# One MLP column group per layer as seven block products instead of eight

## The chip, the cores and the metric

The kernel runs on one core of one Trainium2 chip. Times are device microseconds of one execution. The engines are named as the profile names them: PE (TensorE, matmuls; PEld its weight loads), DVE (VectorE), ACT (ScalarE), POOL (GpSimd) and SP (SyncE, which here issues the DMAs).

## The reference

An encoder of two layers on a sequence of 256 tokens and 1024 channels. Each layer has a token mixer and then the sub-layer that the change touches, a gated MLP of 2816 channels:

```
a, gval = split(xn @ w_up, 2)          # xn: (256, 1024), w_up: (1024, 2 * 2816)
a = depthwise_conv3(a) + conv_b        # over the tokens
h = h + (gelu(a) * gval) @ w_down      # w_down: (2816, 1024)
```

All inputs are float32. `xn` is the RMS-normalized stream, and a final norm follows the second layer.

## The kernel before

*Products.* Every operand of a float32 product is split in two parts, a high part (a cast to the type that TensorE multiplies fast) and a rest (the operand less its high part); a product is three passes, high by high, high by rest and rest by high. The activations stand in `x2`, split once per sub-layer, channels on the partitions: 8 chunks of 128 channels, for each its two parts and two halves `t` of 128 tokens. They are TensorE's stationary operand; the weights stream as the moving one, 512 columns at a time.

*Weights.* Class `Weights` has a list of loads (1 MB each: 512 rows by 512 columns, or 256 rows of 1024) and a list of pieces, two per load (`raw`, ring of three). `get` returns the next piece and splits ahead: a cast by ScalarE (`wh`, L242) and a rest by VectorE (`wl`, L244), into a ring of five buffers. Inside the MLP, where the order of the instructions is written out by hand (`manual_schedule`, `by_hand`), the piece that is split at `get(i)` is piece i + 4, so its cast waits until TensorE is done with piece i - 1. Between the cast and the rest `run_between` puts what stands in `between`.

*The MLP.* Its columns come in groups of 512: five of the activated branch ("a", 0 to 4), five of the gate ("g", 0 to 4), one of the last 256 columns of both ("b"). A group takes four pieces of 12 matmuls (`by_tokens`: two token halves, two chunks of channels, three passes), or 48. Its result, tokens on the partitions, is turned by `to_z` and `cross`: two transposes by VectorE (L744), a DMA to DRAM, four DMAs back (`reads`, held back behind the next load). Then per pair of 128-channel chunks `steps_up` computes the convolution (six activations by ScalarE at L1405 and L1407, two additions by VectorE at L1411 and L1412), the gelu, the gate (L1419) and the split of the product (L1427, L1428). "d" pieces are rows of `w_down`: one piece is 128 channels by 1024 columns and also takes 12 matmuls (L611 to L613), added up over all 22 chunks in four PSUM banks.

`MLP_GROUPS` is the order of all this. Each piece is a place, counted on from 8 behind the first two groups; `PAIR_PLACES` has, for each of the 11 pairs, the places at which its steps are put between or behind the pieces.

*The norm ahead of the MLP.* `to_channels` scales `h` to `xn`, transposes it by TensorE in groups of four chunks (`xt_ps`), and splits each group by a cast (ScalarE, L528) and a rest (VectorE, L529) into `x2`. GpSimd has only the tiny sums and powers of the norms here (L490 to L495) and, at the start, a small table.

Of the kernel before, what the change touches and what calls it, by code (L numbers as in the profile page):

```python
# [10 lines left out]
F32 = mybir.dt.float32  # L11
F32R = mybir.dt.float32r
# [4 lines left out]
P = 128  # L17
# [9 lines left out]
DFF = 2816  # L27
# [24 lines left out]
SEGMENTS = (HALVES, (slice(0, 512), slice(512, 768), slice(768, D)))  # L52

# [51 lines left out]
class Weights:  # L105
# [8 lines left out]
    def __init__(self, tc, pool, idle, small):  # L114
        self.tc, self.nc, self.pool, self.idle, self.small = tc, tc.nc, pool, idle, small
        self.loads, self.pieces = [], []
        self.n_loaded, self.n_split, self.n_got = 0, 0, 0
        self.raw, self.split = {}, {}
        self.live = set()
        self.behind, self.later = (), []  # L120
        self.last, self.rests = [None, None], {}
        self.between = []
        self.loads_behind = {}
        self.n_scaled, self.gains = 0, None
        self.by_hand, self.held_back = 0, []

    def add(self, src, shape, cuts, tag=None):

# [64 lines left out]
    def _split(self, upto):  # L193
        nc = self.nc
        first = self.n_split
        while self.n_split < len(self.pieces):
            i = self.n_split
            n, cut, shape, slot = self.pieces[i]
            if i >= upto and (slot is None or i >= max(upto, first + 2) or i >= upto + 4 or i < 4):
                break  # L200
            if slot is None and len(self.live) == self.BUFS:
                break
            self.load(n + 1)
            with ExitStack() as queued:
                for insts, some in self.later:
                    for inst in insts if i in some else ():
                        if not self.by_hand:
                            queued.enter_context(self.tc.issue_after(inst.ins))
                for hi, lo, *_ in self.open_next():
                    hi()  # L210
                    self.run_between()
                    lo()
            self.load(self.ahead(i))

    def run_between(self):
# [64 lines left out]
def encoder(ctx, tc, x, w_in, w_pool, pool_scale, w_a, w_b, w_o, norm1, norm2, w_up, conv_w,  # L280
# [22 lines left out]
    def of_both(w, r0, c0):  # L303
# [3 lines left out]
            [src[:, :, g] for g in range(2)], (4, 512), [((lambda t, j=j: t[:, 2 * j : 2 * j + 2, :]), (2, 512)) for j in range(2)]  # L307
        )

    first_up = []  # L310
    for l in range(DEPTH):
        for g in range(NG):
# [26 lines left out]
        first_up.append(len(W.pieces))  # L339
        W.use(up + rows(w_up[l], 512, 4, 0, 512), (("v1",), ("ybig",), ("at2",)))  # L340
        for kind, n in MLP_GROUPS:
            if kind == "b":
# [164 lines left out]
    def to_channels(x2, psum, g):  # L507

        tag = "acc" if psum is acc else "mm"

        def fin(t, r, xn):
            for n in range(4):
                cc = slice(n * 256, (n + 1) * 256)
                normed[t] = nc.vector.scalar_tensor_tensor(
                    out=xn[:, cc], in0=h[:, t, cc], scalar=r[:, 0:1], in1=g[:, cc],
                    op0=ALU.mult, op1=ALU.mult,
                )
            for n in range(2):  # L520
                pt = psum.tile([P, 4, P], F32, tag=tag, name="xt_ps")
                ks = slice(4 * n, 4 * n + 4)
                for k in range(4):
                    c0 = (4 * n + k) * P
                    nc.tensor.transpose(pt[:, k, :], xn[:, c0 : c0 + P], ident)  # L525
                oh, ol = (x2[:, ks, part, t, :] for part in (0, 1))
                last = [
                    nc.scalar.copy(out=oh, in_=pt),  # L528
                    nc.vector.tensor_sub(out=ol, in0=pt, in1=oh.bitcast(F32)),  # L529
                ]  # L530
# [154 lines left out]
    def v_tile():  # L685
        return acc.tile([P, 512], F32, tag="acc", name="v_ps")
# [50 lines left out]
    def cross(rows, y, z, name, but=1, after=None):  # L737
# [3 lines left out]

        with tc.issue_after(after.ins) if after and not W.by_hand else ExitStack():
            for t in range(2):
                nc.vector.transpose(out=y[:, t].rearrange("p q c j -> p c q j"), in_=rows[t])  # L744
# [215 lines left out]
    for l in range(DEPTH):  # L960
# [373 lines left out]
                    made = first[i - 2][1]()  # L1334
        W.by_hand = 0
        x2 = two_parts("x", "x2")
        norm = Norm(to_channels(x2, acc, g2))
        entry = []

        def begin_mlp():  # L1340
# [11 lines left out]

        g1 = gain(norm1[l + 1] if l + 1 < DEPTH else norm_f)

        acth, actl = (
            [
                big.tile([P, n, 2, P], F32R, tag=f"{tag}{j}", name=f"act{tag}{j}")
# [1 line left out]
            ]  # L1359
            for tag in "qk"  # L1360
        )
        acts = {}

        zg = big.tile([P, 2, 8, 4, 32], F32, tag="v1", name="zg")
        zga = big.tile([P, 2, 8, 4, 32], F32, tag="xn", name="zga")
        z_of = {(kind, n): z[:, n % 2] for kind, z in (("g", zg), ("a", zga)) for n in range(NQ)}
        z_of["b", 4 * NQ] = big.tile([P, 8, 4, 32], F32, tag="gates", name="zb")

        def branch(kind, f, count=1):

            n, c = divmod(f, 4)
            z, c = (z_of[kind, n], c) if n < NQ else (z_of["b", 4 * NQ], c + 2 * (kind == "g"))
            return z[:, :, c : c + count].rearrange("p (t a) c j -> p c t a j", t=2)

        def to_z(ps, z, *when):
            y = big.tile([P, 2, 4, 4, 32], F32, tag="v0", name="crossing")
            cross(ps, y, z, "crossing", *when)

        held, ps0 = entry
        ps1 = v_tile()
        for n in range(4):
            v_sum(ps1, x2, 1, n, held[n])
        for i, _ in held:
            W.free(i)
        to_z((ps0, ps1), z_of["a", 0], 2, W.behind[1])

        def steps_up(f):

# [76 lines left out]
        to_z(ps, z_of["g", 0], 0, W.last[1])  # L1467
        with tc.manual_schedule():
            W.by_hand = 1
            place, turn = 8, ()  # L1470
            for kind, n in MLP_GROUPS[1:]:
                ps = None
                for i in range(4):
                    if not between and not behind:
                        break
# [4 lines left out]
                    turn = ()  # L1480
                    place += 1
                if kind != "d":
                    turn = (lambda ps=ps, z=z_of[kind, n]: to_z(ps, z),)
# [40 lines left out]
```

## Time and profile before

| | |
|---|---|
| median of 3 runs | 854.8 us (854.66 to 856.39) |
| profiled execution | 854.74 us, of which its span is 853.0 |
| PE, PEld | 99%, 83% of the span busy, 3925 matmul records |
| DVE, ACT, POOL | 71%, 59%, 4% |
| mean DMA rate | 251 GB/s |

A row of the groups by line gives line, engine, operation, written and read tiles, shape and count, then the busy time in us and the mean of one in ns, then the engine's idle time ahead of these and who ended it. A row of a timeline gives start and length in us. A row of the windows view gives a stretch, its length, and the busy time with the count of instructions for PE, PEld, DVE, ACT and POOL, then the granted clock, the DMA engines' share and GB/s. Matmuls overlap, so their spacing is read from the starts.

### The profile page before, as it was taken

The numbers are of one execution on the slowest core, as the hardware profiler recorded it, in microseconds if no ns is written. First come the engines' busy times: TensorE is split into PE (matmuls) and PEld (weight loads), VectorE is DVE, ScalarE is ACT, GpSimd is POOL, SyncE is SP. The second block draws the span as 40 slices with busy tenths as digits, with TensorE's granted clock in tenths as the row PEclk, the third lists the DMA queues.
The fourth block names the chain that finished last, engine by engine and source line by source line (L and its number), as shares of the span: only waits on it lengthen the run. The fifth ranks groups of instructions, "written<-read, shape, count | busy, mean of one in ns | idle before, by whom it ended". The sixth has DMA issues, their size and how long they took to land.

```text
span 853.0 us, 10910 instructions
## 1 busy us (share of the span) xinstructions
PE 846.1 (99%) x3925; PEld 706.7 (83%) x3925; DVE 606.0 (71%) x794; ACT 501.1 (59%) x727; POOL 34.8 (4%) x96
## 2 busy tenths in 40 slices
PE   9999999999999999999999999999999999999997
PEld 7888888888888888888888888888888888888886
DVE  6958877767766776777755687868577767777674
ACT  7744566654543775758545454577454557566682
POOL 1710000000010000000000000000000100000000
PEclk9999999999999999999999999999999999999999
DMA  8698897796747979997726899768777489898931
GB/s 302 213 304 284 302 287 251 250 295 212 249 179 281 280 258 299 285 297 223 243 102 214 261 281 324 252 224 262 244 261 267 145 288 303 248 287 291 296 141 50
DMA packets 147966, 214.03 MB, mean 251 GB/s; under 512 B 7800, under 2 KB 69184, under 8 KB 147912
## 3 DMA queue, kind: packets, MB, share of 16 engines
q1 hardware_dynamic: 147480, 212.67, 76.6%
q8 instruction: 31, 0.51, 0.2%
q10 hardware_dynamic: 432, 0.66, 0.2%
q14 instruction: 23, 0.19, 0.1%
HBM read 186.02 MB, written 27.28 MB: 250 GB/s over the span
## 4 chain that ended last, share of the span: by engine, by line
PE 98%; DVE 1%; ACT 0%; POOL 0%; issue 0%; DVEq 0%; ACTq 0%; POOLq 0%
PE t_ps L694 64%; PE v_ps L694 6%; PE res_ps L611 6%; PE res_ps L612 6%; PE res_ps L613 6%; PE v_ps L940 3%; PE v_ps L839 1%; PE pool_ps L598 1%; PE o_ps L1223 1%; PE s_ps L1175 1%; PE s_ps L1170 1%; PE o_ps L1219 1%; PE xt_ps L525 1%; PE warm_ps L400 0%; PE xt_ps L790 0%; DVE h L505 0%
## 5 line engine op out<-in xcount | busy, mean ns | idle before, releaser
L244 DVE TENSOR_TENSOR wl<-raw,wh 128x1024 fp32r<-128x1024 f32 x274 | 331.7, 1220 | 157.5 <-ACT wh L242 156.4
L694 PE MATMUL t_ps<-wh,x 128*128 128x512 f32 x1408 | 439.2, 390 | 0.0
L242 ACT CAST wh<-raw 128x1024 fp32r<-128x1024 f32 x274 | 285.0, 1049 | 200.6 <-PE t_ps L694 132.0
L694 PEld LDWEIGHTS t_ps<-wh,x 128*128 128x128 f32 x1408 | 264.3, 188 | 55.0
L694 PE MATMUL t_ps<-wl,x 128*128 128x512 f32 x704 | 273.9, 389 | 0.0
L694 PEld LDWEIGHTS t_ps<-wl,x 128*128 128x128 f32 x704 | 132.2, 188 | 27.2
L613 PE MATMUL res_ps<-wh,actk 128*128 128x512 f32 (+1 forms) x184 | 69.8, 380 | 0.0
L611 PE MATMUL res_ps<-wh,actq 128*128 128x512 f32 (+1 forms) x184 | 69.8, 380 | 0.0
L612 PE MATMUL res_ps<-wl,actq 128*128 128x512 f32 (+1 forms) x184 | 69.7, 380 | 0.0
L694 PE MATMUL t_ps<-wh,po 128*128 128x512 f32 x128 | 41.4, 395 | 0.0
L612 PEld LDWEIGHTS res_ps<-wl,actq 128*128 128x128 f32 x184 | 34.6, 188 | 6.7
L613 PEld LDWEIGHTS res_ps<-wh,actk 128*128 128x128 f32 x184 | 34.6, 188 | 6.6
L611 PEld LDWEIGHTS res_ps<-wh,actq 128*128 128x128 f32 x184 | 34.6, 188 | 6.5
L1407 ACT ACTIVATE a<-zga,prm 128x256 f32<-128x256 f32 x80 | 39.0, 514 | 0.0
L490 POOL TENSOR_SCALAR ss<-ss 128x1 f32<-128x1 f32 x8 | 2.1, 266 | 771.9 <-ACT junk L483 771.9
L694 PEld LDWEIGHTS t_ps<-wh,po 128*128 128x128 f32 x128 | 24.1, 188 | 4.9
L611 PE MATMUL res_ps<-wh,m 128*128 128x512 f32 (+1 forms) x72 | 26.5, 368 | 0.0
L612 PE MATMUL res_ps<-wl,m 128*128 128x512 f32 (+1 forms) x72 | 26.3, 365 | 0.0
L744 DVE STREAM_TRANSPOSE crossing<-t_ps 128x512 f32<-128x512 f32 x40 | 26.1, 691 | 0.0
L613 PE MATMUL res_ps<-wh,m 128*128 128x512 f32 (+1 forms) x72 | 26.0, 366 | 0.0
L694 PE MATMUL v_ps<-wh,x 128*128 128x512 f32 x80 | 25.7, 392 | 0.0
L483 ACT ACTIVATE junk<-h 128x512 f32<-128x512 f32 (+1 forms) x19 | 10.5, 554 | 25.2 <-DVE h L505 25.0
(190 smaller groups left out, 923.6 us busy)
## 6 DMA issues: line engine op xcount, KB each, us to landing
raw<-in_w_in_dram SPq DMA_DIRECT2D x58, 1024.0 KB
raw<-in_w_up_dram SPq DMA_DIRECT2D x40, 1024.0 KB
raw<-in_w_down_dram SPq DMA_DIRECT2D x22, 1024.0 KB
crossing<-crossing SPq DMA_DIRECT2D x22, 512.0 KB
crossing<-way SPq DMA_DIRECT2D x16, 512.0 KB
raw<-in_w_a_dram SPq DMA_DIRECT2D x8, 1024.0 KB
raw<-in_w_o_dram SPq DMA_DIRECT2D x8, 1024.0 KB
zga<-crossing SPq DMA_DIRECT2D x40, 128.0 KB
```

The lines of the kernel that those rows point to most:

```text
L242: inst = nc.scalar.copy(out=h, in_=src)
L244: inst = self.rests[i] = nc.vector.tensor_sub(out=l, in0=src, in1=h.bitcast(F32))
L483: nc.scalar.activation(junk[:, 0 : cc.stop - cc.start], h[:, t, cc], AF.Square, scale=D**-0.5, accum_out=ss[:, n : n + 1],)
L525: nc.tensor.transpose(pt[:, k, :], xn[:, c0 : c0 + P], ident)
L598: nc.tensor.matmul(out, w(k), x, start=(steps is first and k == 0), stop=(steps is last and k == nk - 1), skip_group_check=turns["rest"],)
L611: nc.tensor.matmul(ps, ah, wh, start=first, stop=False, skip_group_check=on)
L612: nc.tensor.matmul(ps, ah, wl, start=False, stop=False, skip_group_check=on)
L613: nc.tensor.matmul(ps, al, wh, start=False, stop=last, skip_group_check=on)
L694: nc.tensor.matmul(ps, x2[:, 2 * n + j, part, t, :], w[:, j, :], start=(n + m == 0), stop=(n == last and m == 5),)
L744: nc.vector.transpose(out=y[:, t].rearrange("p q c j -> p c q j"), in_=rows[t])
L940: nc.tensor.matmul(ps[t], a[:, k, t, :], w[:, j, :], start=(k + m == 0), stop=(k == KD - 1 and m == 2),)
L1407: nc.scalar.mul(out=out, in_=a, mul=row(j, c))
```

## The change

In each layer the groups "a 3" and "g 3" become one entry, "w 3". Its weights are a matrix of 1024 rows by 1024 columns, 512 gate and 512 activated columns. It is cut into four quadrants of 512 by 512 ("11" and "21": gate columns, upper and lower channels; "12" and "22": activated columns), the activations into four blocks (two token halves by two halves of the channels). Seven products of blocks, each 4 chunks by 3 passes or 12 matmuls, give the four result blocks that eight gave before. Four of the products (T1 to T4) have a sum of quadrants as weights:

T1 = "12" - "11", T2 = "22" - T1, T3 = "22" - "12", T4 = "21" - T2.

GpSimd computes these in place in the raw tiles, half a quadrant (128x1024) at a time; they are then split like any piece. The sums of blocks of x that go with them are made once per layer behind the norm: `to_channels` keeps whole copies of its transposes (`xf`), VectorE adds them up and splits them (`sum_x`). What the products have in common is added up in PSUM; three copies by ScalarE and two additions by VectorE move parts between banks.

The 14 pieces of products stand in `BLOCK` between the first 8 "d" pieces, which so far were two entries elsewhere, and the places of the pairs' steps change with them. `SUMS` says behind the split of which piece which differences are issued. The first two quadrants are loaded into the tiles `ybig` and `at2`, which are idle there; "22" and "21" go through the ring of three and stay in it until their last difference is made.

```diff
-    ("g", 0), ("a", 1), ("g", 1), ("d", 0), ("a", 2), ("g", 2), ("a", 3), ("g", 3), ("b", 20),
-    ("a", 4), ("g", 4), ("d", 4), ("d", 8), ("d", 12), ("d", 16), ("d", 20),
+    ("g", 0), ("a", 1), ("g", 1), ("a", 2), ("g", 2), ("w", 3), ("b", 20), ("a", 4), ("g", 4),
+    ("d", 8), ("d", 12), ("d", 16), ("d", 20),
...
-    (11, 14), (14, 16), (19, 22), (23, 26), (31, 34), (35, 38), (40, 42), (44, 46), (51, 54), (56, 58), (53, 56),
+    (11, 14), (14, 16), (19, 22), (21, 23), (46, 48), (49, 51), (52, 54), (58, 60), (61, 63), (64, 66), (66, 68),
...
+BLOCK = (
+    ("11", 0), ("11", 1), "d", ("T1", 0), ("T1", 1), "d", ("22", 0), ("22", 1), "d", ("T2", 0), ("T2", 1), "d",
+    ("21", 0), ("21", 1), "d", ("T3", 0), ("T3", 1), "d", "d", ("T4", 0), ("T4", 1), "d",
+)
+SUMS = {
+    ("11", 0): (("T1", 0),), ("11", 1): (("T1", 1),),
+    ("T1", 0): (("T2", 0), ("T3", 0)), ("T1", 1): (("T2", 1), ("T3", 1)),
+    ("T2", 0): (("T4", 0),), ("T2", 1): (("T4", 1),),
+}
...
+        def sum_of(name, j):
+            at = raw(home[name], j)
+            nc.gpsimd.tensor_sub(out=at, in0=raw(of[name], j), in1=at)
...
+                if whole is not None:
+                    nc.scalar.copy(out=whole[:, t, n], in_=pt)
...
+        def sum_x():
+            a11, a12, a21, a22 = (xf[:, t, n] for t in range(2) for n in range(2))
+            nc.vector.tensor_add(out=a22, in0=a21, in1=a22)
+            nc.vector.tensor_sub(out=a21, in0=a11, in1=a21)
+            nc.vector.tensor_sub(out=a11, in0=a22, in1=a11)
+            nc.vector.tensor_sub(out=a12, in0=a12, in1=a11)
+            s = big.tile([P, 2, 2, 2, 4, P], F32R, tag="m2", name="sx")
+            for t in range(2):
+                nc.scalar.copy(out=s[:, t, :, 0], in_=xf[:, t])
+            for t in range(2):
+                nc.vector.tensor_sub(out=s[:, t, :, 1], in0=xf[:, t], in1=s[:, t, :, 0].bitcast(F32))
...
+            bank_of = {"11": "p", "T1": "t", "22": "t", "T2": "q", "21": "p", "T3": "q", "T4": "q"}
...
+            def products(name, j):
+                i, (wh, wl) = W.get()
+                ps = bank(bank_of[name])
+                passes = [(c, part, w) for c in range(2) for part, w in ((0, wh), (0, wl), (1, wh))]
+                for m, (c, part, w) in enumerate(passes):
+                    nc.tensor.matmul(
+                        ps, operands[name](part, 2 * j + c), w[:, c, :],
+                        start=(name in opens and j + m == 0), stop=(j == 1 and m == 5), skip_group_check=True,
+                    )
+                W.free(i)
```

GpSimd's queue in layer 0, between the norm ahead of the MLP and the norm behind it, held before:

```order
L490 TENSOR_SCALAR ss_2210<-ss_2210 128x1
L492 TENSOR_TENSOR ss_2210<-ss_2210 128x1 x2
L495 TENSOR_TENSOR rstd_2323<-ss_2210,mhalf_77 128x1
L490 TENSOR_SCALAR ss_3668<-ss_3668 128x1
L492 TENSOR_TENSOR ss_3668<-ss_3668 128x1
L495 TENSOR_TENSOR rstd_3767<-ss_3668,mhalf_77 128x1
```

Now, with `raw54` for "11" and the home of T1, T2 and T4, `raw55` for "12" and the home of T3, `raw57` for "22" and `raw59` for "21":

```order
L543 TENSOR_SCALAR ss_2211<-ss_2211 128x1
L545 TENSOR_TENSOR ss_2211<-ss_2211 128x1 x2
L548 TENSOR_TENSOR rstd_2326<-ss_2211,mhalf_77 128x1
L344 TENSOR_TENSOR raw54_2719<-raw55_2725,raw54_2719 128x1024 x2
L344 TENSOR_TENSOR raw54_2719<-raw57_2763,raw54_2719 128x1024
L344 TENSOR_TENSOR raw55_2725<-raw57_2763,raw55_2725 128x1024
L344 TENSOR_TENSOR raw54_2719<-raw57_2763,raw54_2719 128x1024
L344 TENSOR_TENSOR raw55_2725<-raw57_2763,raw55_2725 128x1024
L344 TENSOR_TENSOR raw54_2719<-raw59_2944,raw54_2719 128x1024 x2
L543 TENSOR_SCALAR ss_3769<-ss_3769 128x1
```

Eight subtractions stand where nothing stood; T2 and T3 alternate, and T4 comes last.

VectorE's queue in layer 0 at the group "a 3", before (`wl110` to `wl113` are its four pieces, `wl114` is the first of "g 3"):

```order
L744 STREAM_TRANSPOSE crossing_2878<-t_ps_2788 128x4x4x32
L1411 TENSOR_TENSOR y_2865<-y_2865,a0_2864 128x2x255
L1412 TENSOR_TENSOR y_2865<-y_2865,a2_2866 128x2x255
L244 TENSOR_TENSOR wl110_2876<-raw56_2795,wh110_2875 128x1024
L244 TENSOR_TENSOR wl111_2906<-raw56_2795,wh111_2905 128x1024
L1419 TENSOR_TENSOR g_2924<-y_2865,zg_2378 128x512
L244 TENSOR_TENSOR wl112_2922<-raw57_2832,wh112_2921 128x1024
L1428 TENSOR_TENSOR actk1_2377<-g_2924,actq1_2375 128x512
L244 TENSOR_TENSOR wl113_2944<-raw57_2832,wh113_2943 128x1024
L744 STREAM_TRANSPOSE crossing_2964<-t_ps_2873 128x4x4x32
L744 STREAM_TRANSPOSE crossing_2964<-t_ps_2874 128x4x4x32
L244 TENSOR_TENSOR wl114_2962<-raw58_2886,wh114_2961 128x1024
```

Now, from the rest of the 4th entry of `BLOCK` to that of the 12th (`wl109` and `wl110` are T1, `wl115` and `wl116` T2; `raw56` and `raw58` hold "d" weights):

```order
L258 TENSOR_TENSOR wl109_2885<-raw54_2719,wh109_2884 128x1024
L1509 TENSOR_TENSOR actk1_2427<-g_2887,actq1_2425 128x512
L803 STREAM_TRANSPOSE crossing_2909<-t_ps_2802 128x4x4x32
L803 STREAM_TRANSPOSE crossing_2909<-t_ps_2803 128x4x4x32
L258 TENSOR_TENSOR wl110_2907<-raw54_2719,wh110_2906 128x1024
L258 TENSOR_TENSOR wl111_2925<-raw56_2727,wh111_2924 128x1024
L258 TENSOR_TENSOR wl112_2939<-raw57_2763,wh112_2938 128x1024
L258 TENSOR_TENSOR wl113_2963<-raw57_2763,wh113_2962 128x1024
L258 TENSOR_TENSOR wl114_2974<-raw58_2816,wh114_2973 128x1024
L258 TENSOR_TENSOR wl115_2986<-raw54_2719,wh115_2985 128x1024
L258 TENSOR_TENSOR wl116_3005<-raw54_2719,wh116_3004 128x1024
L258 TENSOR_TENSOR wl117_3016<-raw58_2816,wh117_3015 128x1024
```

The rests now follow each other without the steps of pairs between them, and four of these twelve read a tile that GpSimd writes.

More of the change, by code (lines that the diff above doesn't have):

```diff
@@ L125, in __init__ @@
         self.by_hand, self.held_back = 0, []
+        self.sums = {}
     def add(self, src, shape, cuts, tag=None):
@@ L212, in _split @@
                     lo()
+                if i in self.sums:
+                    self.sums.pop(i)()
             self.load(self.ahead(i))
@@ L743, in cross, with to_blocks, send @@
             for t in range(2):
-                nc.vector.transpose(out=y[:, t].rearrange("p q c j -> p c q j"), in_=rows[t])
+                to_blocks(rows[t], y[:, t])
+        return send(y, z, name, but)
+    def to_blocks(rows, y):
+        nc.vector.transpose(out=y.rearrange("p q c j -> p c q j"), in_=rows)
+    def send(y, z, name, but=1):
         d = dram.tile([2 * P, 4, P], F32, tag=name, bufs=2, name=name)
@@ L1361, in encoder @@
         )
[L1362 to L1387, printed above, removed]
         def steps_up(f):
@@ L1472, in encoder @@
                 ps = None
+                if kind == "w":
+                    for make, after in block_units(n):
+                        at_place(place, make, *turn)
+                        place, turn = place + 1, after
+                    continue
                 for i in range(4):
```

107 lines of the change are left out of this document (102 added, 5 removed).

## The prediction

> **What bounds the kernel now.** I read the page first (span, engine shares, chain), then the groups by line, then the timelines of single engines round the MLP, and last each GpSimd row beside what VectorE did at that moment.
>
> ```profile
> span 853.0 us, 10910 instructions
> PE 846.1 (99%) x3925; PEld 706.7 (83%) x3925; DVE 606.0 (71%) x794; ACT 501.1 (59%) x727; POOL 34.8 (4%) x96
> PE 98%; DVE 1%; ACT 0%; POOL 0%; issue 0%; DVEq 0%; ACTq 0%; POOLq 0%
> ```
>
> The chain that ended last is TensorE for 98% of the span: time is the number of matmuls times their spacing as long as nothing makes TensorE wait. The spacing is read from start to start in TensorE's timeline, since the durations (0.39) overlap. These are the first and the last of the 48 matmuls of the "d 0" entry of layer 0:
>
> ```profile
> 290.32 0.39 PE L611 MATMUL res_ps<-wh,actq 128*128 128x512 f32 x1
> ...
> 300.97 0.39 PE L613 MATMUL res_ps<-wh,actk 128*128 128x512 f32 x1
> ```
>
> 10.65 us over 47 steps is 0.2266 us each. So a usual piece of weights (12 matmuls) lasts TensorE 2.72 us, a piece that is used by one product (6) 1.36 us.
>
> What feeds it, by line, and how busy that was while the two entries ran that the change replaces (a stretch of the windows view; columns PE, PEld, DVE, ACT, POOL):
>
> ```profile
> L244 DVE TENSOR_TENSOR wl<-raw,wh 128x1024 fp32r<-128x1024 f32 x274 | 331.7, 1220 | 157.5 <-ACT wh L242 156.4
> L242 ACT CAST wh<-raw 128x1024 fp32r<-128x1024 f32 x274 | 285.0, 1049 | 200.6 <-PE t_ps L694 132.0
> 323.00:344.70 21.70, 21.70 (x97) 17.98 (x96) 14.57 (x17) 13.43 (x20) 0.00 (x0) 1.00 1.04 297
> ```
>
> A piece costs ScalarE 1.05 (cast) and VectorE 1.22 (rest). ScalarE waits mostly for TensorE to free a buffer, VectorE for ScalarE: both run ahead until the buffers are full. VectorE has 14.6 us of work in 21.7, GpSimd none. The cover is the split's lead: four pieces, 10.9 us.
>
> **The change part by part.**
>
> *Products.* Per layer 96 matmuls become 84. The program's own order counts 24 fewer on TensorE in all, and nothing added: 24 x 0.2266 = 5.4 us off, all of it on the path. Each layer also splits 14 pieces for 16; both engines have room, so that is worth nothing.
>
> *Where the seven products run.* Their 14 pieces stand among 8 pieces of the down projection: 22 units that last TensorE 84 x 0.2266 + 96 x 0.2266 = 40.8 us (counted from 1: T1 is units 4 and 5, T2 10 and 11, T3 16 and 17, T4 20 and 21; units 3, 6, 9, 12, 15, 18, 19 and 22 are "d"). Two product units and one "d" take 5.4 us, in which VectorE must make three rests (3.7), so far well.
>
> *The differences.* Eight GpSimd subtractions of 128x1024 per layer, which no row of this trace shows. The nearest ones:
>
> ```profile
> L443 POOL COPY fsb<-rbt 4x11 f32<-4x11 f32 x1 | 0.2, 188 | 0.0
> L448 POOL COPY fsb<-fsb 4x128 f32<-4x128 f32 x1 | 0.3, 279 | 0.0
> ```
>
> From 11 to 128 elements a copy grows by 91 ns, 0.78 ns an element: 1024 elements with one operand would be 188 + 1013 x 0.78, 1.0 us, the lower end. A second operand fetched after the first makes it 1.8; if the write came in series too it would be 2.6, the upper end. Nothing in the rows decides between the last two; I take the middle, 2.2.
>
> The Trainium skill (GPSIMD Engine Reference, Performance versus the Vector engine) has 4497 ns for such an add of 2048 elements; half of it, 2.25, is an estimate from that page which no run here shows, and the sum below would be 864.5 by it. Its section Engine selection gives elementwise work on two tensors to VectorE, against this change.
>
> *What they meet.* GpSimd's few rows of before say more than their lengths:
>
> ```profile
> 241.50 0.57 POOL L495 TENSOR_TENSOR rstd<-ss,mhalf 128x1 f32<-128x1 f32 x1
> 247.23 1.21 DVE L244 TENSOR_TENSOR wl<-raw,wh 128x1024 fp32r<-128x1024 f32 x1
> 247.41 1.46 POOL L495 TENSOR_TENSOR rstd<-ss,mhalf 128x1 f32<-128x1 f32 x1
> 427.42 0.19 POOL L492 TENSOR_TENSOR ss<-ss 128x1 f32<-128x1 f32 x1 [1.78 <-ACT junk L483]
> 428.99 1.22 DVE L244 TENSOR_TENSOR wl<-raw,wh 128x1024 fp32r<-128x1024 f32 x1
> 429.06 1.21 POOL L492 TENSOR_TENSOR ss<-ss 128x1 f32<-128x1 f32 x1 [1.44 <-ACT junk L483]
> ```
>
> The same tiny instruction takes 0.57 alone and 1.46 when a rest runs; another 0.19 and 1.21. The second ends at 430.27, the rest at 430.21: GpSimd stood still until VectorE's instruction on two SBUF tensors was through. It can last over several such instructions:
>
> ```profile
> L443 POOL COPY fsb<-rbt 4x8 f32<-4x8 f32 x1 | 2.6, 2633 | 0.0
> 28.67 1.41 DVE L255 SCALAR_TENSOR_TENSOR wl<-raw,gcol,wh 128x512 fp32r<-128x512 f32 x2
> 30.00 0.68 DVE L922 TENSOR_TENSOR x<-xu,x 128x512 fp32r<-128x512 f32 x1
> 30.60 0.68 DVE L820 TENSOR_TENSOR xu<-xuh,xul 128x512 f32<-128x512 f32 x1
> ```
>
> A copy of 8 elements lasted 2.63 us over these four. So the two engines take turns at a path to SBUF. The rows show GpSimd waiting; that VectorE waits as long for a difference they can't show, since GpSimd's instructions were all short. I take it to hold both ways.
>
> The Trainium skill (SBUF — State Buffer, SBUF: two separate sides) calls that pair of ports an exclusive lock, held for a whole instruction by whichever began first. Its direction GpSimd-waits agrees with the 1.21 beside 0.19 us above; by its other direction the sum is the forecast's, without it the first rival's.
>
> *The ledger of that path, per layer.* VectorE's other customers of it are the steps of a pair of channel chunks; a transpose holds VectorE, though not the path:
>
> ```profile
> L1412 DVE TENSOR_TENSOR y<-y,a 128x510 f32<-128x510 f32 x22 | 15.2, 692 | 2.3
> L1411 DVE TENSOR_TENSOR y<-y,a 128x510 f32<-128x510 f32 x22 | 14.9, 676 | 12.9 <-ACT y L1405 12.9
> L1419 DVE TENSOR_TENSOR g<-y,zg 128x512 f32<-128x512 f32 x20 | 13.6, 681 | 0.0
> L1428 DVE TENSOR_TENSOR actk<-g,actq 128x512 fp32r<-128x512 f32 x22 | 15.0, 684 | 0.0
> L744 DVE STREAM_TRANSPOSE crossing<-t_ps 128x512 f32<-128x512 f32 x40 | 26.1, 691 | 0.0
> L1407 ACT ACTIVATE a<-zga,prm 128x256 f32<-128x256 f32 x80 | 39.0, 514 | 0.0
> L1405 ACT ACTIVATE y<-zga,prm 128x256 f32<-128x256 f32 x40 | 24.1, 601 | 0.0
> ```
>
> I count from the moment the first difference can start to the moment TensorE reaches unit 12. There is time for: the lead of 10.9, less the first quadrant's own cast and rest (2.3), less the six activations of a pair that ScalarE has ahead of that cast (4 x 0.51 + 2 x 0.60, some 3): 5.6 us; and TensorE's units 1 to 11, eight of 1.36 and three of 2.72: 19.0. Together 24.6 us. In it fall the rests of units 2 to 12 (11 x 1.22 = 13.4), six pair steps (6 x 0.68 = 4.1) and two transposes (1.4, of which half may lie beside a difference: 0.7): 18.2. Six differences are ready in that time too (two T1, two T2, two T3): 6 x 2.2 = 13.2. That is 31.4 of work in 24.6: TensorE waits 6.8 us per layer. At 1.0 a difference it would be nothing, at 1.8 it is 4.4, at 2.6 it is 9.2. Behind unit 12 the remaining two differences, ten rests and five transposes and additions (4.4 + 12.2 + 3.5 = 20.1) fit into TensorE's 21.8. So 13.6 us for two layers, of which the 5.4 pay a part.
>
> Who waits: a T unit's cast stands in ScalarE's queue behind nothing but its difference, so the casts behind it wait as well, and with them VectorE's rests; and the third load of "d" weights on SP's queue now waits for T3's second difference, with all later loads behind it.
>
> *Sums of x.* Four additions (4 x 0.69), two rests (2 x 1.22) and two casts after the norm, 5.2 us of VectorE. They stand between the first rests of the MLP, six of which have 16.3 us of TensorE time: 7.3 + 5.2 + four transposes 2.8 = 15.3. It fits; nothing, at most 2 a layer without the lead.
>
> *Four more PSUM copies in the norm.* These stand in ScalarE's queue where TensorE has little in hand:
>
> ```profile
> 244.95 0.68 DVE L529 TENSOR_TENSOR x<-xt_ps,x 128x512 fp32r<-128x512 f32 x1
> 246.00 0.59 ACT L528 CAST x<-xt_ps 128x512 fp32r<-128x512 f32 x1 [0.70 <-PE xt_ps L525]
> 248.91 1.67 DVE L516 SCALAR_TENSOR_TENSOR xn<-h,rstd,gain 128x256 f32<-128x256 f32 x4 [0.46 <-POOL rstd L495]
> 249.94 0.60 PE L525 MATMUL xt_ps<-ident,xn 128*128 128x128 f32 x4
> ```
>
> The first copy comes behind the rest that ends at 245.63 and lasts like the cast beside it, 0.59: the next cast moves from 246.0 to 246.2, and the square, the sum and xn behind it. Half of xn (two of four, 0.8 us) is there at 249.75, its transposes run at 249.94: 0.2 of room for a shift of 0.2 to 0.8. Between 0 and 0.8; 0.5 a layer, 1.0 in all. The block's three PSUM copies and two additions stand behind units with 2.7 us to spare: nothing.
>
> *Sum.* The profiled execution took 854.74 (span 853.0 and 1.7 around it; the median of the runs is 854.8): 854.74 - 5.4 + 13.6 + 1.0 = 863.9.
>
> **The rivals.**
>
> *All hidden, faster.* If VectorE doesn't wait for GpSimd, or a difference is as short as the copy's slope (1.0), only the products and the norm are left: 854.74 - 5.4 + 1.0 = 850.3. For it: GpSimd's waits are the only direction shown. Against: two engines that take turns one way have to share something. It decides at a difference of (24.6 - 18.2) / 6 = 1.07 us; up to 1.43 the wait (2.2 a layer) still costs no more than the gain.
>
> *VectorE keeps the path.* The 2.63 us copy shows that rests in a row can shut GpSimd out. Then the differences come last, and the wait is a load's:
>
> ```profile
> DMA packets 147966, 214.03 MB, mean 251 GB/s; under 512 B 7800, under 2 KB 69184, under 8 KB 147912
> ```
>
> With the rests of 13 units (15.9), the pair steps (4.1) and six differences (13.2), T3 is done 33.2 after the start, 27.6 after TensorE's unit 1. A load of 1 MB at 251 GB/s (4.2), its cast and rest (2.3): unit 15 would start at 34.1 for 24.5. 9.6 a layer: 854.74 - 5.4 + 19.2 + 1.0 = 869.5. Against: most GpSimd rows end with the first instruction that held them.
>
> *A tie.* Differences of about 1.4 us, gain and wait equal: 854 to 855.5.
>
> **How the numbers follow.** Forecast 864 with 0.66; its own range, 1.8 to 2.6 a difference with the norm at 0 to 0.8, is 858 to 870. VectorE keeps the path 0.14, all hidden 0.15, a tie 0.05. I give 850 to 875: both rivals lie in it, and about a tenth lies beyond, mostly above, where late loads come on top. A difference of 0.2%, 1.7 us, is about what a measurement of this kernel tells from none. Faster 0.15, same 0.05, slower 0.80.
>
> **What would show it.** Right: 24 fewer matmul records; differences of 2 us and more, some lengthened by the rest before them; rests of well over 1.22 us in the block; TensorE idle some 5 to 9 us per layer, released by the rests of the T units or the "d" units between. Wrong: rests that stay at 1.22 beside a running difference (first rival); TensorE idle at unit 15 behind a DMA (second); differences near 1 us; idle time at the norms beyond 1 us, which would mean that the copies and the sums of x were under-priced.

## The result

The changed kernel takes 867.19 us (median of 4 runs, 866.62 to 868.43) against 854.93 before (median of 4, 854.66 to 856.39): 1.0141 times as long, 95% interval 1.0128 to 1.0153. It is slower, 3 us above the forecast of 864.0 and inside the range. The profiled execution took 866.62 with a span of 864.8, so the 11.8 us between the spans is what the traces have to account for.

In the changed kernel the rest of a split is L258 (cast L256), the GpSimd difference L344, the block's products L1578, the "d" matmuls L666 to L668, the transposes L803, and the addition of the down projection to the stream L558. From its page: the span, the busy time of the engines, the chain that ended last by engine, and three groups by line.

```profile
span 864.8 us, 10958 instructions
PE 843.9 (98%) x3901; PEld 700.8 (81%) x3901; DVE 659.1 (76%) x822; ACT 524.5 (61%) x757; POOL 83.6 (10%) x112
PE 87%; DVE 7%; issue 3%; ACT 1%; DMA 1%; POOL 0%; DVEq 0%; ACTq 0%; POOLq 0%
L258 DVE TENSOR_TENSOR wl<-raw,wh 128x1024 fp32r<-128x1024 f32 x286 | 370.5, 1314 | 113.0 <-ACT wh L256 112.1
L344 POOL TENSOR_TENSOR raw<-raw,raw 128x1024 f32<-128x1024 f32 x16 | 49.3, 3099 | 130.5 <-DVE wl L258 130.5
L803 DVE STREAM_TRANSPOSE crossing<-t_ps 128x512 f32<-128x512 f32 x36 | 23.9, 694 | 6.8 <-DMA crossing<-crossing 6.8
```

The 24 matmuls are gone (3925 to 3901), and TensorE has left a tenth of the chain to others, most of it to VectorE. The rests have become longer by 0.094 us on average: 286 times that is 27 us of VectorE's time. GpSimd hardly appears in the chain: it works 49 us on its differences, and the harm is read from VectorE's rows. The transposes wait for nothing but 6.8 us, for a buffer.

What TensorE itself waits for, from the waits view of the changed kernel (us in total, times, longest), has three kinds of rows above 1 us:

```profile
PE t_ps L1578 <- DVE wl L258: 5.8, 8, 1.7
PE res_ps L667 <- DVE wl L258: 4.2, 3, 1.7
PE xt_ps L578 <- DVE xn L569: 1.7, 1, 1.7
```

The first two are the block, products and the "d" pieces between them, and one "d" piece behind the block's last products. All wait directly for rests, none for a DMA. The timelines of GpSimd, VectorE and TensorE in the block of layer 0 show how a wait comes about (start and length in us; the three engines' rows stand one behind the other):

```profile
304.66 2.41 POOL L344 TENSOR_TENSOR raw<-raw,raw 128x1024 f32<-128x1024 f32 x1 [55.78 <-DVE wl L258]
315.90 2.79 POOL L344 TENSOR_TENSOR raw<-raw,raw 128x1024 f32<-128x1024 f32 x1 [4.89 <-DVE wl L258]
318.67 3.37 POOL L344 TENSOR_TENSOR raw<-raw,raw 128x1024 f32<-128x1024 f32 x1
321.99 3.37 POOL L344 TENSOR_TENSOR raw<-raw,raw 128x1024 f32<-128x1024 f32 x1
...
305.08 3.06 DVE L258 TENSOR_TENSOR wl<-raw,wh 128x1024 fp32r<-128x1024 f32 x1 [0.50 <-ACT wh L256]
316.35 1.31 DVE L803 STREAM_TRANSPOSE crossing<-t_ps 128x512 f32<-128x512 f32 x2
317.58 2.21 DVE L258 TENSOR_TENSOR wl<-raw,wh 128x1024 fp32r<-128x1024 f32 x1
319.71 3.41 DVE L258 TENSOR_TENSOR wl<-raw,wh 128x1024 fp32r<-128x1024 f32 x1
323.04 3.40 DVE L258 TENSOR_TENSOR wl<-raw,wh 128x1024 fp32r<-128x1024 f32 x1
329.69 1.21 DVE L258 TENSOR_TENSOR wl<-raw,wh 128x1024 fp32r<-128x1024 f32 x1
...
321.10 0.40 PE L666 MATMUL res_ps<-wh,actq 128*128 128x512 f32 x1
323.17 0.50 PE L667 MATMUL res_ps<-wl,actq 128*128 128x512 f32 x1 [1.67 <-DVE wl L258]
```

The first difference finds the path free: 2.41. The rest behind it (305.08) takes 3.06 and ends at 308.14, 1.07 behind the difference's end. From 317.58 on the two engines alternate: the rest that begins at 319.71 ends at 323.12; the difference that begins at 321.99 ends at 325.36, 2.24 behind that; the next rest ends at 326.44, 1.08 behind the difference. Each instruction's recorded length holds the other's turn. A pair takes 3.33 us (319.71 to 323.04), and rests alone follow each other by 1.14 (329.69, and the next at 330.83), so one difference takes 2.2 us from VectorE. The transposes lie wholly beside a difference and stay at 0.65 each. At 321.10 TensorE begins unit 6, a "d" piece, with its first matmul, whose weights are the high part; the second needs the rest that ends at 323.12, and starts at 323.17.

The Trainium skill (SBUF — State Buffer, SBUF: two separate sides) has this pair of ports as an exclusive lock on which the loser blocks for a whole instruction; the trace now agrees for both directions, 3.41 for a rest of 1.22 and 3.37 for a difference of 2.41.

The busy time in the same stretch before and after (columns: us, PE, PEld, DVE, ACT, POOL, granted clock, DMA share, GB/s), from the windows view of each:

```profile
318.50:331.00 12.50, 12.50 (x57) 10.36 (x56) 7.95 (x8) 5.00 (x6) 0.00 (x0) 1.00 1.03 306
```

```profile
318.50:331.00 12.50, 8.15 (x32) 5.46 (x31) 12.50 (x6) 5.74 (x7) 10.19 (x4) 1.00 0.60 171
```

VectorE looks busy all through with 6 instructions where 8 took 7.95 us: it stands in line, and TensorE is busy two thirds of the time. The loads fall back as well (306 to 171 GB/s), but TensorE waits for none of them; a kernel below in which TensorE doesn't wait in the block at all has 163 GB/s in the same stretch.

Three more things changed: the block's last unit, the "d" piece 22 (TensorE 356.14, 357.44), the norm behind layer 0 (429.55, 431.56), and the end. Timelines of the changed kernel, a piece for each, VectorE's row first where there is one:

```profile
355.57 0.72 DVE L803 STREAM_TRANSPOSE crossing<-t_ps 128x512 f32<-128x512 f32 x1 [3.96 <-DMA crossing<-crossing]
356.14 0.39 PE L666 MATMUL res_ps<-wh,actq 128*128 128x512 f32 x1
357.44 0.50 PE L667 MATMUL res_ps<-wl,actq 128*128 128x512 f32 x1 [0.91 <-DVE wl L258]
...
429.55 0.28 PE L668 MATMUL res_ps<-wh,actk 128*128 128x256 f32 x1
431.56 0.44 PE L578 MATMUL xt_ps<-ident,xn 128*128 128x128 f32 x2 [1.73 <-DVE xn L569]
...
853.04 0.69 DVE L558 TENSOR_TENSOR h<-res_ps,h 128x512 f32<-128x512 f32 x1 [2.42 <-PE res_ps L668]
856.42 0.28 PE L668 MATMUL res_ps<-wh,actk 128*128 128x256 f32 x1
```

And the end before:

```profile
840.40 0.69 DVE L505 TENSOR_TENSOR h<-res_ps,h 128x512 f32<-128x512 f32 x1 [1.84 <-PE res_ps L613]
846.58 0.28 PE L613 MATMUL res_ps<-wh,actk 128*128 128x256 f32 x1
```

At 355.57 the block's second transposed half waits 3.96 us in VectorE's queue for the tile that the first half still leaves by DMA, and the rest behind it comes late. At the norm the first transposes start 2.01 us behind the matmul ahead of them; before it was 0.29 (424.91 and 425.20). The first of the last four additions to the stream (the L558 and L505 rows) began 6.2 us ahead of the last matmul before and 3.4 ahead of it now, and from the last matmul to the end it is 8.4 us (864.8 - 856.42) for 6.4 (853.0 - 846.58).

The account in the profiled execution: products -5.4; block waits with the slow restart behind each, 6.1 in layer 0 (units 1 to 21 start at 311.94 and end at 356.14, for 14 x 1.36 + 7 x 2.72 = 38.1 us of matmuls) and 6.2 in layer 1 (read from the start of the MLP and its last matmul); the late unit 22 1.2, in layer 0 alone; the norm behind layer 0 1.7; the end 2.0; the norm ahead of the MLP -0.1 (the MLP's first matmul starts at 257.54, at 257.68 before). Together 11.7 of the 11.8 between the spans. (The first expectation below takes 6.0 for the block and 1.9 for the norm.)

### The profile page after: what moved, and what is told of

Read it like the earlier page. It is cut to its first block, busy times and chain, and to the rows that moved or that the text cites. A ratio compares the mean times of both kernels' runs of the same rounds, so it can differ in the third digit from the quotient of the medians.

```text
span 864.8 us, 10958 instructions
## 1 busy us (share of the span) xinstructions
PE 843.9 (98%) x3901; PEld 700.8 (81%) x3901; DVE 659.1 (76%) x822; ACT 524.5 (61%) x757; POOL 83.6 (10%) x112
## 4 chain that ended last, share of the span: by engine, by line
PE 87%; DVE 7%; issue 3%; ACT 1%; DMA 1%; POOL 0%; DVEq 0%; ACTq 0%; POOLq 0%
PE t_ps L749 55%; PE v_ps L749 6%; PE res_ps L667 5%; PE res_ps L666 5%; PE res_ps L668 5%; DVE wl L258 4%; PE v_ps L1002 3%; PE t_ps L1578 2%; PE pool_ps L653 1%; PE v_ps L901 1%; PE o_ps L1285 1%; PE s_ps L1237 1%; DVE y L1492 1%; ACT wh L256 1%; PE s_ps L1232 1%
## 5 line engine op out<-in xcount | busy, mean ns | idle before, releaser
L258 DVE TENSOR_TENSOR wl<-raw,wh 128x1024 fp32r<-128x1024 f32 x286 | 370.5, 1314 | 113.0 <-ACT wh L256 112.1
L256 ACT CAST wh<-raw 128x1024 fp32r<-128x1024 f32 x286 | 297.4, 1049 | 188.6 <-PE t_ps L749 102.8
L749 PE MATMUL t_ps<-wh,x 128*128 128x512 f32 x1280 | 399.7, 390 | 0.0
L749 PEld LDWEIGHTS t_ps<-wh,x 128*128 128x128 f32 x1280 | 240.3, 188 | 49.8
L749 PE MATMUL t_ps<-wl,x 128*128 128x512 f32 x640 | 249.1, 389 | 0.0
L749 PEld LDWEIGHTS t_ps<-wl,x 128*128 128x128 f32 x640 | 120.2, 188 | 24.9
L666 PE MATMUL res_ps<-wh,actq 128*128 128x512 f32 (+1 forms) x184 | 70.0, 381 | 0.0
L668 PE MATMUL res_ps<-wh,actk 128*128 128x512 f32 (+1 forms) x184 | 69.1, 381 | 0.0
L344 POOL TENSOR_TENSOR raw<-raw,raw 128x1024 f32<-128x1024 f32 x16 | 49.3, 3099 | 130.5 <-DVE wl L258 130.5
L667 PEld LDWEIGHTS res_ps<-wl,actq 128*128 128x128 f32 x184 | 34.6, 188 | 12.3 <-DVE wl L258 5.7
L666 PEld LDWEIGHTS res_ps<-wh,actq 128*128 128x128 f32 x184 | 34.6, 188 | 6.8
L668 PEld LDWEIGHTS res_ps<-wh,actk 128*128 128x128 f32 x184 | 34.6, 188 | 6.4
L1492 DVE TENSOR_TENSOR y<-y,a 128x510 f32<-128x510 f32 x22 | 19.3, 878 | 13.5 <-ACT y L1486 13.5
L803 DVE STREAM_TRANSPOSE crossing<-t_ps 128x512 f32<-128x512 f32 x36 | 23.9, 694 | 6.8 <-DMA crossing<-crossing 6.8
L666 PE MATMUL res_ps<-wh,m 128*128 128x512 f32 (+1 forms) x72 | 26.5, 368 | 0.0
L668 PE MATMUL res_ps<-wh,m 128*128 128x512 f32 (+1 forms) x72 | 26.0, 366 | 0.0
```

The source lines that it names most:

```text
L256: inst = nc.scalar.copy(out=h, in_=src)
L258: inst = self.rests[i] = nc.vector.tensor_sub(out=l, in0=src, in1=h.bitcast(F32))
L344: nc.gpsimd.tensor_sub(out=at, in0=raw(of[name], j), in1=at)
L666: nc.tensor.matmul(ps, ah, wh, start=first, stop=False, skip_group_check=on)
L667: nc.tensor.matmul(ps, ah, wl, start=False, stop=False, skip_group_check=on)
L668: nc.tensor.matmul(ps, al, wh, start=False, stop=last, skip_group_check=on)
```

## The experiments

All ratios are against the kernel before, run beside each experiment on the same chip (median 854.88 for the first four, 854.80 for the last four).

**No differences.** Everything else of the change stays.

```diff
         def sum_of(name, j):
             at = raw(home[name], j)
-            nc.gpsimd.tensor_sub(out=at, in0=raw(of[name], j), in1=at)
+            pass
```

> The eight subtractions per layer are left out, so T1 to T4 take the weights that stand in their tiles and the result isn't the reference's; splits, products, places and the order stay. Theory (GpSimd and VectorE exclude each other at SBUF): the waits of TensorE inside the block, 6.0 us a layer in the trace of after, go. Left are the products (-5.4) and the three places that the forecast didn't have, at the crossing (1.2), at the norm behind layer 0 (1.9) and at the end (2.0): 854.9 - 5.4 + 5.1 = 854.6. Rival A (the waits come from product units that last half as long for the same split): it stays near 867. Rival B (the three other places are backlog of the block): 849.5.

Measured 853.16 (853.01 to 853.43), ratio 0.9976 [0.9967, 0.9986]. The block's waits are gone; the waits view of this kernel and its line of rests:

```profile
PE xt_ps L578 <- DVE xn L569: 1.7, 1, 1.7
L258 DVE TENSOR_TENSOR wl<-raw,wh 128x1024 fp32r<-128x1024 f32 x286 | 345.2, 1219 | 128.8 <-ACT wh L256 125.9
DVE crossing L803 <- DMA crossing<-crossing: 5.6, 2, 2.8
```

The rests are back at 1.219. All of 14.0 us hangs on the eight subtractions a layer. Two costs stay that have nothing to do with GpSimd: the norm behind layer 0 (1.7) and the end (last matmul 842.87, span 851.3: 8.4). The third, the 1.2 at unit 22, went too, which puts the time 1.4 below the theory's 854.6. The transposes still wait for their buffer, 2.8 us in each layer, but TensorE doesn't feel that; nor does it in layer 1 of the changed kernel, where the wait is 2.81. It is the 1.1 us more of layer 0 there (3.96) that reaches TensorE, and why that transfer took longer is not shown.

**The same differences on VectorE.** Same places, same operands.

```diff
-            nc.gpsimd.tensor_sub(out=at, in0=raw(of[name], j), in1=at)
+            nc.vector.tensor_sub(out=at, in0=raw(of[name], j), in1=at)
```

> The same subtractions by VectorE in the place of GpSimd. Theory: the shared path now carries 1.22 for a difference instead of 2.2. By the forecast's ledger 18.2 + 0.7 (transposes can lie beside nothing) + 6 x 1.22 = 26.2 in 24.6, 1.6 a layer: 867.2 - 12.0 + 3.2 = 858.4. Rival (what costs is the long way of a T piece over GpSimd and back, not the path): the way is 1 us shorter and VectorE is slowed by nobody, 855 or less.

Measured 860.44 (859.54 to 861.32), ratio 1.0058 [1.0035, 1.0081]: 6.8 us faster than on GpSimd, 2 slower than expected. A difference takes 1.2 there. One wait a layer is left, at unit 6, whose rest stands in VectorE's queue behind two pairs of differences. What I had missed is what comes after the wait (windows view, the wait and the 3.5 us behind it):

```profile
320.00:323.00 3.00, 1.11 (x6) 0.61 (x5) 3.00 (x4) 1.91 (x3) 0.00 (x0) 1.00 0.14 53
323.80:327.30 3.50, 3.50 (x10) 2.68 (x10) 3.50 (x4) 0.29 (x1) 0.00 (x0) 0.51 0.93 308
```

The granted clock falls to 0.51 in this stretch and TensorE runs some eight matmuls at 0.43 each instead of 0.23: 1.6 us beside the 2.05 of the wait itself.

**GpSimd work that nobody reads, in the kernel before.** Sixteen subtractions of the same size per layer, put behind the split of the first piece of "a 3"; the order on all other engines is that of the kernel before.

```diff
+    def idle_work(first):
+        out = big.tile([P, 2, 512], F32, tag="ybig", name="idle")
+        nc.gpsimd.tensor_sub(out=out, in0=W.raw[first][:, 0:2], in1=W.raw[first][:, 0:2])
+        for _ in range(15):
+            nc.gpsimd.tensor_sub(
+                out=out, in0=h[:, 0].rearrange("p (a b) -> p a b", a=2),
+                in1=h[:, 1].rearrange("p (a b) -> p a b", a=2),
+            )
...
+                    if (kind, n, j) == ("a", 3, 0):
+                        W.sums[len(W.pieces)] = lambda first=len(W.loads): idle_work(first)
...
```

> The kernel before with 16 GpSimd subtractions of 128x1024 per layer whose result nobody reads, started with the first half of group a 3; every other engine's instructions and order are those of before. Theory: 16 x 2.2 = 35.2 us of the path. While they alternate with VectorE's instructions (some 51 us) VectorE has 0.67 x 51 = 34 of its own work; 69.5 in 51 and a lead of 8.6 is 10 us of waiting a layer: 854.9 + 20 = 875, and rests of 3.4 us beside them. Rival (a GpSimd difference costs only through those who wait for its result): 855.

Measured 885.45 (885.1 to 885.94), ratio 1.0351 [1.0329, 1.0372]. Nothing depends on these results, and still the kernel takes 31 us more. From the groups by line (30 of the 32 subtractions, those that read `h`) and the waits view:

```profile
L317 POOL TENSOR_TENSOR idle<-h 128x1024 f32<-128x1024 f32 x30 | 91.7, 3057 | 2.4
L247 DVE TENSOR_TENSOR wl<-raw,wh 128x1024 fp32r<-128x1024 f32 x274 | 368.6, 1357 | 131.9 <-ACT wh L245 131.0
PE t_ps L708 <- DVE wl L247: 20.1, 18, 3.6
```

The direction that the trace of before could not show, VectorE waiting for GpSimd, is there without anything else of the change. Nor is it a load that TensorE waits for: while the subtractions run, VectorE is busy for all but 0.1 us from 312 to 356. It is 10 us above what I expected; TensorE's eighteen waits account for 20.1 us, and a stretch behind one of them ran at a clock of 0.62:

```profile
335.00:339.00 4.00, 4.00 (x12) 3.08 (x12) 4.00 (x2) 0.92 (x1) 3.92 (x2) 0.62 0.00 0
```

The rest of the 30.6 us between the spans is close to what follows the waits. A wait costs some 0.27 us beyond its idle time: the matmul at 325.40 was due at 323.36, 2.04 us earlier, of which 1.88 count as idle, and the next one follows after 0.34 for 0.23. For eighteen waits I estimate 4.9 us from this. Three stretches of 3.4 us at half the clock cost up to 1.7 each, 5.1. With the waits that makes 30.1.

**The places of the last pairs' steps earlier.** GpSimd's differences stay.

```diff
-    (11, 14), (14, 16), (19, 22), (21, 23), (46, 48), (49, 51), (52, 54), (58, 60), (61, 63), (64, 66), (66, 68),
+    (11, 14), (14, 16), (19, 22), (21, 23), (46, 48), (48, 50), (51, 53), (54, 56), (58, 61), (60, 62), (62, 64),
```

> The kernel after with the steps of the last pairs put earlier: (48, 50), (51, 53), (54, 56), (58, 61), (60, 62), (62, 64) for the last six. The block stays as it is. Theory (the waits at the norm behind layer 0 and at the end come from the late places of the pairs, which keep VectorE from the norm and let the last held pieces fall behind): both go, 3.9 us: 863.3. Rival (they are lag of the block that VectorE never makes up): 867.

Measured 864.72 (863.25 to 866.75), ratio 1.0116 [1.0085, 1.0147]. The waits view keeps the block and loses the norm:

```profile
PE t_ps L1578 <- DVE wl L258: 5.9, 8, 1.7
PE res_ps L667 <- DVE wl L258: 4.1, 3, 1.7
PE xt_ps L578 <- DVE xn L569: 0.2, 1, 0.2
```

The first of the last four additions begins 6.0 us ahead of the last matmul again (849.13 and 855.09), and the end is back at 6.4 us. So 1.5 of the norm's 1.7 us and the end's 2.0 belong to the new places of the last pairs, 3.3 us of the span (861.5). The medians differ by 2.5: the four executions took 863.25, 863.41, 866.04 and 866.75, and the trace is of the first of these.

**No differences and the earlier places together.** The edits of the first and the fourth experiment.

> No differences (the result isn't the reference's) and the pairs' places of the earlier run together: what seven products are worth with nothing in their way. Theory (the products' 5.4 us are there in full, the sums of x and the four PSUM copies cost nothing): 854.9 - 5.4 = 849.5, up to 0.5 more for what is left of the wait at the norm behind layer 0. Rival (the forecast's price of the norm copies, 0.5 a layer, or a wait at the sums of x): 850.5 or more.

Measured 850.24 (849.78 to 854.64), ratio 0.9955 [0.9940, 0.9969]. The rest of the change without its two costs is worth 4.6 of the 5.4 us. The time lies between the theory's 849.5 to 850.0 and the rival's 850.5. The trace of this kernel is of an execution that took 854.64, where the other five took 849.78 to 851.03: in it the next layer's loads came late, the norm waited 1.8 us again, and the clock was halved behind it. It doesn't speak for the median; the two kernels that follow have the earlier places too, and wait 0.2 at that norm.

**Differences on VectorE, spread out.** The earlier places; each difference behind a later split, so that not more than one stands ahead of a rest; another tile for the block's second crossing.

```diff
-    ("T1", 0): (("T2", 0), ("T3", 0)), ("T1", 1): (("T2", 1), ("T3", 1)),
-    ("T2", 0): (("T4", 0),), ("T2", 1): (("T4", 1),),
+    ("22", 0): (("T2", 0),), ("22", 1): (("T2", 1),), ("T2", 0): (("T3", 0),), ("T2", 1): (("T3", 1),),
+    ("21", 0): (("T4", 0),), ("21", 1): (("T4", 1),),
...
-            nc.gpsimd.tensor_sub(out=at, in0=raw(of[name], j), in1=at)
+            nc.vector.tensor_sub(out=at, in0=raw(of[name], j), in1=at)
...
-                    kept["y"] = big.tile([P, 2, 4, 4, 32], F32, tag="v0", name="crossing")
+                    kept["y"] = big.tile([P, 2, 4, 4, 32], F32, tag="v0" if kind == "a" else "at2", name="crossing")
```

> Differences by VectorE, issued later (T2 behind the splits of quadrant 22, T3 behind T2, T4 behind quadrant 21), the earlier places, and the second crossing of the block in a tile of its own: meant to beat both kernels. Theory: in the stretch to unit 12 VectorE now has 18.9 + 6 x 1.22 = 26.2 at most, but T3 falls behind it: 18.9 + 4 x 1.22 = 23.8 in 24.6, no wait; and over the block 41.5 of VectorE for 40.8 plus the lead. 849.5 + 0 to 2 = 851. Rival (one queue in order, each T piece needs three turns of cast, difference and rest: waits of 2 us and the halved clock behind them stay): 856.

Measured 849.92 (849.77 to 850.03, 5 runs), ratio 0.9941 [0.9928, 0.9955]: faster than both kernels. Its page, and the stretch of the block in the windows view:

```profile
span 848.1 us, 10952 instructions
L344 DVE TENSOR_TENSOR raw<-raw,raw 128x1024 f32<-128x1024 f32 x16 | 19.4, 1215 | 0.1
318.50:331.00 12.50, 12.50 (x57) 10.36 (x56) 12.50 (x12) 7.66 (x9) 0.00 (x0) 1.00 0.58 163
```

VectorE is as full in this stretch as in the changed kernel, but with 12 instructions instead of 6, and TensorE never waits in the block.

**The same on GpSimd.** The one word `vector` in the line of the difference is `gpsimd` again; all else is as in the kernel above.

> The same with the differences on GpSimd again. Theory: to unit 12 only T1 and T2 fall, 18.2 + 4 x 2.2 = 27.0 in 24.6: 2.4 a layer; T3 and T4 behind it are 8.8 + 12.2 + 3.5 = 24.5 in 21.8 and what lead is left, another 0 to 2.7. 849.5 + 2 x (2.4 to 5.1) = 854.3 to 859.7, about 857. Rival (alternation stretches eight rests by 2.2 wherever they lie, so spreading doesn't help): 862, the earlier run with these places.

Measured 862.33 (861.8 to 862.82), ratio 1.0086 [1.0073, 1.0100]. The theory's 857 was wrong and the rival's 862 right: spreading, with the other tile, gains 2.4 us on the fourth experiment. The groups and the waits:

```profile
L344 POOL TENSOR_TENSOR raw<-raw,raw 128x1024 f32<-128x1024 f32 x16 | 50.2, 3157 | 130.0 <-DVE wl L258 73.6 <-DMA raw<-in_w_up_dram 56.3
PE t_ps L1578 <- DVE wl L258: 5.4, 6, 1.7
PE res_ps L667 <- DVE wl L258: 3.3, 2, 1.7
```

In the alternation a difference takes its 2.2 us from VectorE here too; with eight of them a layer between rests that TensorE needs at its own rate, a lead like the changed kernel's 7 us (304.66 to the block's first matmul at 311.94) doesn't hold them. Between this kernel and the one above the engine of sixteen instructions is the only edit: 12.4 us.

**Copies in place of the differences.** One operand instead of two, on GpSimd, at the change's own places.

```diff
-            nc.gpsimd.tensor_sub(out=at, in0=raw(of[name], j), in1=at)
+            nc.gpsimd.tensor_copy(out=at, in_=raw(of[name], j))
```

> The kernel after with a copy by GpSimd (one operand, 128x1024) in the place of each subtraction, so the result isn't the reference's. By the slope of the copies in the trace of before a copy is 1.0: 18.2 + 6.0 = 24.2 in 24.6, no wait of its own; 853.2, as without differences, up to 855. Rival (a GpSimd instruction of this size costs the same whatever it reads, about 2.2): 867.

Measured 853.23 (853.06 to 854.81), ratio 0.9982 [0.9973, 0.9991], as with no differences at all. From the line's own view (shortest, median and longest in ns) and the groups:

```profile
L344 POOL COPY raw<-raw x16: 1039/1442/2033, 304.8 to 745.7; 128x1024 f32<-128x1024 f32 x16
L258 DVE TENSOR_TENSOR wl<-raw,wh 128x1024 fp32r<-128x1024 f32 x286 | 353.3, 1249 | 119.6 <-ACT wh L256 116.4
```

The shortest copy, 1.04, is the prediction's lower end (188 + 1013 x 0.78 ns) to 0.06. The copies do meet the rests, the longest of which takes 2.07 us here, but the rests grow by 0.03 on average and TensorE waits for none. So GpSimd's work in these places isn't harmful as such; instructions that hold the path for about 1.0 us each fit. The copy differs from the difference in its operands as well as its length, and no run has a length between 1.04 and 2.4, so the prediction's turning point of 1.07 us is borne out from its lower side alone.

## Why the prediction was right, and where it was not

*Products, -5.4.* Right: 24 records fewer, and without GpSimd's differences and the late places the kernel gains 4.6 (fifth experiment), with VectorE's 4.9.

*The difference, 2.2 between 1.0 and 2.6.* A difference that finds the path free takes 2.40, one in the alternation takes 2.2 from VectorE. The lower end was the price of a copy, measured 1.04; the difference with its second operand takes 1.4 more, so neither "1.8" nor "2.6" was the mechanism. By the Trainium skill (GPSIMD Engine Reference, Performance versus the Vector engine) the estimate was 2.25, and the shortest trace record is 7% above it. Its section Engine selection spoke against GpSimd for such work, and the pair of spread kernels agrees, 849.92 to 862.33.

*VectorE waits as GpSimd does.* This was taken without a row that showed it and decided the sign. The idle work in the kernel before and the rests of 3.41 show it; the first rival (all hidden, 850.3) falls with it.

*The ledger, 13.6.* The mechanism was right; the size was 12.3 with the restarts. Two entries were off in opposite ways. The time was too short: the first difference starts 7.3 us ahead of the block (304.66 and 311.94), not 5.6, which alone takes the wait through unit 12 from 6.8 to 5.1 a layer; TensorE's loss up to there is 5.6 in the trace (unit 12 starts at 336.55, where 311.94 and 19.0 us of matmuls give 330.94). And behind unit 12, where I had said that all fits, the two T4 differences cost another 0.5: the rests beside them (333.10 and 336.44) take 3.4 each, and the second is the one that unit 13 waits for. The stretch was right as a sum but too coarse for a queue in which every pair has its date.

*Copies in the norm, 1.0.* Wrong, they cost nothing: the MLP of layer 0 starts 0.14 us earlier than before, and in layer 1 it is 244.01 us from the first mixer product that follows the norm's transposes (440.26) to the MLP (684.27), for 243.99 before (433.91 to 677.90). The 0.2 us of room that I read there was enough, or the shift smaller; which of the two I did not try. The sums of x cost nothing, as priced.

*What no step had.* Three waits of 4.9 us together, each in a place where the change moves work without adding any. The pairs' new places put the last steps and two held pieces so late that the norm behind layer 0 waits 1.7 more and the end grows by 2.0; the fourth experiment shows that. Idle time at a norm was to be a sign of underpriced copies; this one went with the places and the copies stayed. The 1.2 at unit 22 lie in the stretch behind unit 12 where the prediction said that all fits: its sum has VectorE's busy time, and not a transpose that waits in VectorE's queue for its tile. The moved places are named ahead of the prediction, which priced nothing for them. Together with the smaller ledger and the norm: 863.9 - 1.3 - 1.1 + 4.9 = 866.4, for the 866.62 of the profiled execution. That the forecast came within 3 us is in part luck: what it counted too much makes up for half of what it didn't see.

*The rivals.* VectorE does not keep the path: where both queues hold work (from 317.58 to 328) the turns are one and one, no wait at unit 15 is there, and no wait of TensorE in the block ends with a DMA. The tie needed 1.4 us a difference and is excluded with 2.2.

## What to carry to other kernels

Work given to an "idle" engine is free only if it shares nothing with the busy one, or no more than that one has to spare (the copies of 1.04 us): price a GpSimd instruction on two SBUF tensors by what it takes from VectorE's two-tensor instructions (here 2.2 us where VectorE itself needs 1.2), before counting GpSimd's idle time. A ledger over a stretch gives sign and size when a shared resource is overfull; the waits themselves sit at the pieces with the shortest notice, and have to be checked piece by piece. When a change reorders hand-placed steps, look at both ends of the reordered sequence, since what comes late there is paid in the next norm and in the tail even where no work was added.

## What the runs showed of the hardware that I had not expected

A wait of TensorE below 2 us can halve the clock behind it. In the kernel with the differences on VectorE at the change's own places, the timeline of TensorE has one wait in the block and then matmuls at twice the spacing:

```profile
320.53 0.39 PE L666 MATMUL res_ps<-wh,actq 128*128 128x512 f32 x1
322.81 0.50 PE L667 MATMUL res_ps<-wl,actq 128*128 128x512 f32 x1 [1.89 <-DVE wl L258]
...
324.64 0.63 PE L667 MATMUL res_ps<-wl,actq 128*128 128x512 f32 x1
325.07 0.63 PE L668 MATMUL res_ps<-wh,actk 128*128 128x512 f32 x1
```

The idle time is 1.89 us here (1.88 in layer 1, with a clock of 0.55 in the stretch from 746.80 to 750.30 behind it). In the changed kernel waits of 1.67 in the block and 1.73 at the norm leave the clock at 1.00, as the windows behind two of them show:

```profile
431.50:435.00 3.50, 3.44 (x25) 3.27 (x26) 3.23 (x8) 1.93 (x5) 0.27 (x2) 1.00 0.14 55
323.50:327.00 3.50, 3.18 (x14) 2.34 (x13) 3.50 (x2) 0.96 (x1) 3.50 (x2) 1.00 0.76 222
```

The Trainium skill (TensorE: Matmul & The Clock Gate, What's actually happening) gives an idle window of about 3.4 us ahead of such a fall; here 1.89 was enough.

The length of one wait does not decide alone. In the kernel with the idle GpSimd work a wait of 1.88 us, up to 325.40, leaves the clock at 1.00 (from 322 to 330). The clock records of the ten traces show what else counts. In each trace the times at which the granted clock changes lie whole multiples of 3.413 us apart, and a fall ahead of a kernel's end lasts one such step: the two in the kernel with the differences on VectorE begin at 323.90 and 747.15, 124 steps apart. TensorE's idle time can be added up over these steps, by the ends that the profile gives for its matmuls. At full clock, every step with 1.88 us or more of it was followed by half the clock, and none with 1.73 or less; between these lie one of 1.79 that was followed by it (fifth experiment) and one of 1.85 that was not (at the end of the first). The wait up to 325.40 falls into two steps, 0.84 and 1.04. So the same wait can cost its length or 1.7 us more, by where it falls on this grid.
